# Norm factors formed in rows and spread over the partitions through DRAM

## The chip, the cores and the metric

The kernel runs on one core of a Trainium2 chip. The metric is the device time of one execution in microseconds (us). The kernel before takes 2180.92 us, the median of three runs. The profile shows five engines: TensorE (PE, with its weight loads shown apart as PEld), VectorE (DVE), ScalarE (ACT), GpSimd (POOL), and SyncE (SP), whose queue issues the transfers (SPq).

## The reference

A decoder trunk of two layers on one sequence of 1024 positions and width 1024. Every sub-layer is preceded by an RMS norm, `y = x * rsqrt(mean(x*x) + eps) * g`, and followed by a residual addition:

```
for layer in (0, 1):
    hn = rms_norm(h, mix_norm[layer])
    h = h + (rg_lru_block(hn, ...) if layer == 0 else stick_breaking_attention(hn, w_qkv, w_o))
    h = h + swiglu_ffn(rms_norm(h, ffn_norm[layer]), ffn_w_in[layer], ffn_w_out[layer])
return rms_norm(h, final_norm)

swiglu_ffn(x):  gu = x @ w_in;  (silu(gu[:, :2816]) * gu[:, 2816:]) @ w_out
```

The attention has 16 heads of 64: scores z = q k / 8, from them weights by a suffix product of sigmoids, then weights times v. All is float32; a product is formed of a high and a low part of each operand (fp32r), in three matmuls.

## The kernel before, in words

**Layout.** The activations stand transposed: channels on the partitions (8 blocks `d` of 128), positions along the rows in two halves `n` of 512. `h[d][n]` is the residual, 128x512. The norm's factor belongs to a position, so it is the same on all partitions and differs along the row. It is not applied to the activations ahead of a matmul but to its result: the projections run on `h * g`, and the result is multiplied with the factors where it leaves PSUM. So the factors are needed in the form [128, 512] per half, the same row on every partition.

**Forming the factors.** The squares of h are added over the blocks d into `acc[0]` and `acc[1]` (128x512 each; in the attention into `rbc[0]`, `rbc[1]`), by `squares` (L212: ACT squares, POOL or DVE adds). What is left is the sum over partitions, the root, and the spreading. Before, `stats_mm` (L952) does it for a feed-forward block: for every 128 positions a matmul with the squares as stationary operand and a column of ones as moving one, which puts the sums of 128 positions into one column of `half(ob, 1)`, 128x8 in all; then `rstd` (L178: one ACT root, five DVE instructions on 128x8) into `rcol`. `factors` (L965) spreads them: for every 128 positions a matmul whose stationary operand is the column of `rcol`, broadcast, and whose moving one is the identity, 128x128 each, into the PSUM tile `ob`. One such float32 matmul is two PE instructions in the profile. The attention does the same by halves with `stats` (L202) and `broadcast_r` (L188), and copies the result to `rbc[n]`.

**The feed-forward block** (`mix_out_ffn_in`, L629). The mixer's output projection adds into h; meanwhile the seven operands of a Strassen-like product are formed (`v_steps`, `v_last`). The input projection then runs in steps of 128 channels f; step f needs seven products `i`, in the order 0, 1, 2, 3, 4, 6, 5 (`ORDER`), each 12 matmuls of 128x512. Step 0 is written apart: six products without their last block (L924), the last blocks of these one after another (L926 on, k = 0 to 5), then product 6. Then come the steps f = 1 to 21 in one loop (L1122, `s_` = 0, 1, ...), k counting the seven products. After every product its result is evacuated (`post`) and a piece of the weight work for the next step is issued: a step's weights are the parts `wa` (products 0, 1), `wb` (2, 4), `wc` (3, 5), `wd` (6), each with a high half cast by ACT (`a_hi` L708, `b_hi` L717, `c_hi`, `d_hi`) and a low half by DVE (`a_lo` L712, `b_lo` L721, `c_lo`, `d_lo`); `wb` comes from sums `sb` that DVE forms (L695 to L704). A step's `b_lo` is issued at the start of that step, after the gate of the step before.

`gate` multiplies a step's result with `ob` on DVE (L889), takes Silu on ACT (L891), multiplies again (L893) and with the other branch (L895). The gate of step 0 runs at k = 5 and 6 of `s_` = 0, so `ob` must hold the factors by then.

The last four squares of h are left over when step 0 begins. Before, they run after k = 0 and k = 1 of `s_` = 0, two each, with the adds on DVE (L1172); `stats_mm` follows at k = 3, `factors` at k = 5.

**The attention** starts with the q, k and v columns of the first pair of heads. `qkv_steps` (L1415) gives 3 matmuls at a time; the loop at L1637 counts them (i = 1 to 34), and the table `between` (L1629) says what is put after which: sums of squares of half 0 at 12 and of half 1 at 16, spreading at 17 and 21, and `waiting[0]`, `waiting[1]`, the evacuation of the two q halves, at 18 and 22. `evacuate` (L1445) multiplies with `rbc[n]` on DVE (`t`, L1459), splits into `two` (ACT L1467, DVE L1468; two buffers), and SP spreads it to the tiles `q` (L1471, L1472) and `kk` (L1475) by four transfers. After i = 34 the chunks begin: `z_part` (L1508, two banks in `psZ`), then the sigmoid on ACT that frees the bank (L1521).

**Order.** In both places the order on PE, ACT, DVE and POOL is the order of the program text (`manual_schedule`). In the attention's part that holds for SP too; in the feed-forward block SP's order is the planner's. Every engine runs its list in order: what stands behind a waiting instruction waits as well.

Of the kernel before, what the change touches and what calls it, by code (L numbers as in the profile page):

```python
# [8 lines left out]
F32 = mybir.dt.float32  # L9
# [3 lines left out]
AF = mybir.ActivationFunctionType  # L13
ALU = mybir.AluOpType
PSUM = bass.MemoryType.PSUM

P = 128
S = 1024
D = 1024
ND = D // P  # L20
NT = S // P
# [12 lines left out]
def trunk(  # L34
# [59 lines left out]
    nc.gpsimd.memset(ones, 1.0)  # L94
    eps4 = cp.tile([P, 1], F32, name="eps4")
    nc.gpsimd.memset(eps4, 0.25 * EPS)
    vc = cp.tile([P, P], F32, name="vc")

    rbc = [cp.tile([P, NB], F32, name=f"rbc{n}") for n in range(NH)]
# [7 lines left out]
            for d in range(ND):  # L107
                x_[d] = [xp.tile([P, NB], F32R, name=f"{nm}{d}_{n}") for n in range(NH)]
    rcol = cp.tile([P, NT], F32, name="rcol")
    cp.tile([P, 136], F32, name="edge_l")  # L110


    def load_raw(src, shape):
# [64 lines left out]
    def rstd(dst, sums):  # L178
        n = dst.shape[-1]
        quarter, root = (cp.tile([P, max(n, 4)], F32, tag=x, name=x, bufs=2)[:, 0:n] for x in ("rs_m", "rs_s"))  # L180
        nc.scalar.activation(root, sums, AF.Sqrt, scale=0.25 / D, bias=eps4)
        nc.vector.tensor_scalar(quarter, sums, 0.25 / D, 0.25 * EPS, op0=ALU.mult, op1=ALU.add)
        nc.vector.reciprocal(dst, root)
        nc.vector.tensor_mul(quarter, quarter, dst)
        nc.vector.tensor_add(quarter, quarter, root)
        nc.vector.reciprocal(dst, quarter)

    def broadcast_r(ps_pool, tag, n):  # L188
        ps = ps_pool.tile([P, NB], F32, tag=tag, name="rb_ps")
        for i in range(4):  # L190
            b = 4 * n + i
            nc.tensor.matmul(
                ps[:, i * P : (i + 1) * P],
                lhsT=rcol[:, b : b + 1].broadcast_to([P, P]),
                rhs=ident,
                start=True,
                stop=True,
            )
        nc.vector.tensor_copy(rbc[n], ps)


    def stats(acc, ps_pool, tag, n, i0=0, i1=4):  # L202
        ps = ps_pool.tile([P, NB], F32, tag=tag, name="st_ps")
        accs = acc if isinstance(acc, tuple) else (acc,)
        for i in range(i0, i1):
            for a in accs:
                nc.tensor.matmul(
                    ps[:, i : i + 1], lhsT=a[:, i * P : (i + 1) * P], rhs=ones, start=a is accs[0], stop=a is accs[-1]
                )
        rstd(rcol[:, 4 * n + i0 : 4 * n + i1], ps[:, i0:i1])  # L210

    def squares(h, d, n, sqp, acc, eng=None, first=None):  # L212
        if d == 0 if first is None else first:
            nc.scalar.square(acc[n], h[d][n])
        else:
            sq = sqp[n % len(sqp)] if isinstance(sqp, list) else sqp.tile([P, NB], F32, tag="sq", name="sq", bufs=2)
            nc.scalar.square(sq, h[d][n])
            (eng or nc.gpsimd).tensor_add(acc[n], acc[n], sq)
# [410 lines left out]
    def mix_out_ffn_in(h, mix, bias, layer, gnext, outs):  # L629
# [141 lines left out]
        with tc.manual_schedule(engines={E.PE, E.Activation, E.DVE, E.Pool}):  # L771
# [154 lines left out]
            for k, i in enumerate(ORDER0[:6]):  # L926
                part(P0[i], w, i, rhs_in[i], (HK - 1,))
                if k == 1:
                    w.d_hi()
                    w.d_lo()  # L930
                elif k == 3:
                    nw.a_hi()
                elif k == 5:
                    nw.a_lo()
                if k < 5:
                    post0(i, P0[i])
# [12 lines left out]
            nw.ready = True  # L949


            def stats_mm():  # L952
                st_ps = half(ob, 1)
                for n in range(NH):
                    for i in range(4):
                        nc.tensor.matmul(
                            st_ps[:, 4 * n + i : 4 * n + i + 1],
                            lhsT=acc[n][:, i * P : (i + 1) * P],
                            rhs=ones,
                            start=True,  # L960
                            stop=True,
                        )
                rstd(rcol, st_ps[:, 0:NT])

            def factors():  # L965
                for b in range(NT):
                    nc.tensor.matmul(
                        ob[:, b * P : (b + 1) * P],
                        lhsT=rcol[:, b : b + 1].broadcast_to([P, P]),
                        rhs=ident,  # L970
                        start=True,
                        stop=True,
                    )


            VISITS = (
# [145 lines left out]
            for s_, (kind, x) in enumerate(steps):  # L1122
# [21 lines left out]
                for k, i in enumerate(ORDER):  # L1144
# [22 lines left out]
                        for dn in old:  # L1167
                            finished(*dn)
                    if s_ == 0:
                        if k < 2:  # L1170
                            for _ in range(2):
                                squares(h, *sq_todo.pop(0), rbc, acc, V)  # L1172
                        elif k == 3:
                            stats_mm()
                        elif k == 5:
                            factors()
# [189 lines left out]
    with ExitStack() as st:  # L1366
# [48 lines left out]
        def qkv_steps(q):  # L1415
            for which in range(3):
                w, at = wq.pop((q, which)), 3 * q + which + 1
                if at < 3 * NP:
                    wq[divmod(at, 3)] = next_weights(raws.pop(at))
                else:  # L1420
                    mix[0].w[mix[0].order[0]] = next_weights(mix[0].raw.pop(0))
                for i in (at + 1,) if at < 3 * NP else (at + 1, at + 2):
                    load_link(i)

                ks = (1, 5, 2, 6, 3, 7, 0, 4) if (q, which) == (0, 0) else range(ND)
                for n in range(NH):
                    pool, tag = (psZ, "z") if (q, which) == (0, 0) else (psQ, "qk")
                    ps = pool.tile([P, NB], F32, tag=tag, name="qk_ps")
                    for i, k in enumerate(ks):
                        mm3(ps, w[0][:, k], w[1][:, k], xh[k][n], xl[k][n], i == 0, i == ND - 1)  # L1430
                        if i == 5 and late:
                            late.pop()()
                        if i < ND - 1:
                            yield
                    ev = evacuate(q, which, n, ps)
                    if (q, which) == (0, 0):
                        waiting.append(ev)
                        yield
                    else:
                        next(ev)  # L1440
                        yield
                        next(ev, None)
# [181 lines left out]
        with tc.manual_schedule(engines={E.PE, E.Activation, E.DVE, E.Pool, E.SP}):  # L1624


            load_link(1)
            first = qkv_steps(0)
            between = {  # L1629
                12: lambda: stats(rbc[0], psO, "o", 0),  # L1630
                16: lambda: stats(rbc[1], psO, "o", 1),
                17: lambda: broadcast_r(psO, "o", 0),
                18: lambda: [*waiting[0]],
                21: lambda: broadcast_r(psO, "o", 1),
                22: lambda: [*waiting[1]],
            }
            for i in range(1, 2 * ND * NH + 3):  # L1637
                next(first)
                if i in between:
                    between[i]()  # L1640
                if i > 4 and later:
                    later.pop(0)()

            gains = [len(units) - x for x in (31, 29, 27)]

            last_two, out_work = len(units) - 2 * 12, out_fill()
            amount = {x: 2 for x in (-1, 0, 1, 9, 10, 11, 12)}
            amount.update({x: 1 for x in range(14, 21)})
            c = 0
            for u in range(-LEAD, len(units)):  # L1650
                some = chunks[c : c + 1]
                c += 1
                for a in some:
                    z = z_part(*a)
                if 0 <= u + 2 < len(units):
                    ready[u + 2] = t_split(t_part(*units[u + 2]), *units[u + 2])
                for a in some:
                    z_rest(z, *a)
                if u - last_two == 1:
                    late.pop()()  # L1660
                if u - last_two == 9:
                    mix[0].w[mix[0].order[1]] = next_weights(mix[0].raw.pop(1), nc.gpsimd)
                if later:
                    later.pop(0)()
                for _ in range(2):
                    next(fill, None)
                for _ in range(amount.get(u - last_two, 0)):
                    next(out_work)
                if u in gains:
                    z_rest(z_part(*chunks[c]), *chunks[c])  # L1670
                    c += 1
                if u >= 0:
                    av_part(ready.pop(u), *units[u])
            while later:
                later.pop(0)()
# [48 lines left out]
```

## Time and profile before

| what | us |
|---|---|
| median of the runs | 2180.92 |
| lowest and highest of 3 runs | 2179.82, 2181.77 |
| span of the profiled execution, first to last instruction | 2179.1 |
| PE busy | 2165.8 |
| DVE busy | 1701.4 |
| ACT busy | 1079.8 |
| POOL busy | 113.5 |

The profile gives the profiled execution only as its span; the runs' times lie 0.7 to 2.7 above it. TensorE's granted clock is 1.000 over the span.

In a timeline row the first number is the start in us from the span's start, the second the duration, then engine, line of the kernel, operation, out<-in and the shape of the output; x16 says that 16 instructions stand in one row; brackets give the idle time of the engine before the row and what ended it. In the rows of a line or tile the three numbers behind the count are the shortest, median and longest duration in ns. In the rows of transfers the last number is the us from issue to landing. Consecutive instructions overlap by 0.05 to 0.1 us in their recorded times, and a matmul's recorded duration holds its way through the array: its price is the distance from one start to the next.

### The profile page before, as it was taken

To read this page: it belongs to the slowest core of one execution; us is meant where nothing else is said; L and a number is where in the kernel's file an instruction comes from. 1 tells how busy PE (TensorE), PEld (TensorE's weight loads), DVE (VectorE), ACT (ScalarE), POOL (GpSimd) and SP (SyncE) were. 2 spreads that over 40 slices of the span, in tenths; PEclk is the share of its full clock that TensorE was granted. 3 is DMA by queue.
4 is the path that set the end of the run, shared out by engine and by line. 5 is a ranking of instruction groups with operands and counts; after the bars stand their busy time and mean duration, and the time that the engine had idled before them with its cause. 6 is when DMAs were issued, how large, how long until landed. Compare 5 with 4: busy or idle time off the path is not lost.

```text
span 2179.1 us, 27430 instructions
## 1 busy us (share of the span) xinstructions
PE 2165.8 (99%) x10126; PEld 1802.7 (83%) x10126; DVE 1701.4 (78%) x2380; ACT 1079.8 (50%) x1765; POOL 113.5 (5%) x85
## 2 busy tenths in 40 slices
PE   9999999999999999999999999999999999999998
PEld 7888888888888888888888888888888888888887
DVE  7888777767777887887888888886877777788886
ACT  6677445434444544564555555553543444454556
POOL 1222020000000000000000000002000000000002
PEclk9999999999999999999999999999999999999999
DMA  7111412344444764434333344552133444467452
GB/s 233 49 49 39 135 39 73 102 126 157 138 146 139 247 222 130 145 120 101 100 96 94 95 105 107 143 194 60 52 115 122 147 145 141 144 229 234 138 153 92
DMA packets 296101, 277.64 MB, mean 127 GB/s; under 512 B 15256, under 2 KB 210976, under 8 KB 295968
## 3 DMA queue, kind: packets, MB, share of 16 engines
q1 hardware_dynamic: 295808, 275.64, 40.8%
q8 instruction: 79, 1.29, 0.2%
q14 instruction: 54, 0.44, 0.1%
q10 hardware_dynamic: 160, 0.27, 0.0%
HBM read 175.71 MB, written 74.97 MB: 115 GB/s over the span
## 4 chain that ended last, share of the span: by engine, by line
PE 90%; DVE 6%; ACT 3%; DMA 1%; issue 1%; SPq 0%; DVEq 0%; ACTq 0%
PE p_ps L145 18%; PE p_ps L143 18%; PE p_ps L144 18%; PE qk_ps L143 4%; PE qk_ps L145 4%; PE qk_ps L144 4%; PE wt_ps L1538 3%; PE ob_ps L143 3%; PE ob_ps L144 2%; PE ob_ps L145 2%; PE z_ps L1508 2%; PE z_ps L1509 2%; PE av_ps L1560 2%; PE av_ps L1559 1%; PE a_ps L144 1%; PE a_ps L145 1%
## 5 line engine op out<-in xcount | busy, mean ns | idle before, releaser
L145 PE MATMUL p_ps<-vh,wal 128*128 128x512 f32 x524 | 204.1, 389 | 0.1
L143 PE MATMUL p_ps<-vh,wch 128*128 128x512 f32 x524 | 204.2, 390 | 0.0
L145 PE MATMUL p_ps<-vh,wbl 128*128 128x512 f32 x524 | 204.1, 390 | 0.0
L145 PE MATMUL p_ps<-vh,wcl 128*128 128x512 f32 x524 | 204.1, 390 | 0.0
L143 PE MATMUL p_ps<-vh,wbh 128*128 128x512 f32 x524 | 204.1, 390 | 0.0
L144 PE MATMUL p_ps<-vl,wbh 128*128 128x512 f32 x524 | 203.9, 389 | 0.0
L144 PE MATMUL p_ps<-vl,wch 128*128 128x512 f32 x524 | 203.9, 389 | 0.0
L143 PE MATMUL p_ps<-vh,wah 128*128 128x512 f32 x524 | 203.9, 389 | 0.0
L144 PE MATMUL p_ps<-vl,wah 128*128 128x512 f32 x524 | 203.9, 389 | 0.0
L1547 ACT CAST th<-wt_ps 128x512 fp32r<-128x512 f32 x192 | 92.5, 482 | 209.0 <-PE wt_ps L1538 208.8
L717 ACT CAST wbh<-sb 128x1024 fp32r<-128x1024 f32 (+2 forms) x69 | 69.8, 1011 | 192.9 <-DVE sb L701 192.9
L1548 DVE TENSOR_TENSOR tl<-wt_ps,th 128x512 fp32r<-128x512 f32 x192 | 106.0, 552 | 63.0 <-ACT th L1547 61.2
L143 PE MATMUL qk_ps<-vh,whi 128*128 128x512 f32 x264 | 118.3, 448 | 0.0
L145 PEld LDWEIGHTS p_ps<-vh,wbl 128*128 128x128 f32 x524 | 98.4, 188 | 21.4 <-DVE wbl L721 1.0
L145 PEld LDWEIGHTS p_ps<-vh,wal 128*128 128x128 f32 x524 | 98.3, 188 | 21.4 <-DVE wal L712 1.0
L145 PEld LDWEIGHTS p_ps<-vh,wcl 128*128 128x128 f32 x524 | 98.4, 188 | 21.0 <-DVE wcl L731 0.6
L143 PEld LDWEIGHTS p_ps<-vh,wch 128*128 128x128 f32 x524 | 98.4, 188 | 20.5 <-ACT tb L1106 0.2
L144 PEld LDWEIGHTS p_ps<-vl,wah 128*128 128x128 f32 x524 | 98.4, 188 | 20.4
L144 PEld LDWEIGHTS p_ps<-vl,wbh 128*128 128x128 f32 x524 | 98.4, 188 | 20.4
L144 PEld LDWEIGHTS p_ps<-vl,wch 128*128 128x128 f32 x524 | 98.4, 188 | 20.4
L143 PEld LDWEIGHTS p_ps<-vh,wah 128*128 128x128 f32 x524 | 98.4, 188 | 20.4
L143 PEld LDWEIGHTS p_ps<-vh,wbh 128*128 128x128 f32 x524 | 98.4, 188 | 20.2
(356 smaller groups left out, 5574.1 us busy)
## 6 DMA issues: line engine op xcount, KB each, us to landing
raw<-in_ffn_w_in SPq DMA_DIRECT2D x88, 512.0 KB, 3.9
vl<-pd SPq DMA_DIRECT2D x128, 256.0 KB, 3.9
pd<-U SPq DMA_DIRECT2D x90, 256.0 KB, 2.3
kk<-two SPq DMA_DIRECT2D x64, 256.0 KB, 3.9
raw<-in_ffn_w_out SPq DMA_DIRECT2D x56, 256.0 KB, 3.5
raw<-in_attn_w_qkv SPq DMA_DIRECT2D x24, 512.0 KB, 4.0
q<-two SPq DMA_DIRECT2D x64, 128.0 KB, 2.3
raw<-in_lru_w_in SPq DMA_DIRECT2D x15, 512.0 KB, 3.9
```

The lines of the kernel that those rows point to most:

```text
L143: nc.tensor.matmul(ps, lhsT=wh, rhs=mh, start=first, stop=False, **kw)
L144: nc.tensor.matmul(ps, lhsT=wh, rhs=ml, start=False, stop=False, **kw)
L145: nc.tensor.matmul(ps, lhsT=wl, rhs=mh, start=False, stop=last, **kw)
L717: nc.scalar.copy(self.full(self.wb), self.full(self.sb))
L1508: nc.tensor.matmul(ps[:, 0 : c1 - c0], lhsT=lhsT, rhs=KK[q][hx][:, 0, c0:c1], start=True, stop=False)
L1509: nc.tensor.matmul(ps[:, 0 : c1 - c0], lhsT=lhsT, rhs=KK[q][hx][:, 1, c0:c1], start=False, stop=True)
L1538: nc.tensor.transpose(tp[:, c : c + P], W[q, hx, j, kb // 4][:, (kb % 4) * P : (kb % 4 + 1) * P], ident)
L1547: nc.scalar.copy(th[:, q0:], tp[:, q0:])
L1548: nc.vector.tensor_sub(tl[:, q0:], tp[:, q0:], f32(th)[:, q0:])
L1559: nc.tensor.matmul(ps[:, q0:], lhsT=VV[q][:, kb, hx], rhs=th[:, q0:], start=first, stop=False)
L1560: nc.tensor.matmul(ps[:, q0:], lhsT=VV[q][:, kb, hx], rhs=tl[:, q0:], start=False, stop=last)
```

## The change

`row_stats` forms the sums as rows: a matmul per 128 positions with a stationary operand of eight columns, of which column b is ones and the others zero (cut out of `pick`), and the squares as the moving operand. All add up in one 8x128 area of PSUM (4x128 in the attention), row b holding the 128 sums of block b. The root and the five DVE instructions then work on 8x128, and SP writes the result to DRAM. `row_back` reads 512 factors of it back, the same to all 128 partitions. In the feed-forward blocks `factors` is then two ACT copies from `rbc[n]` to `ob` and no matmul.

Places: the last four squares of a feed-forward block move to k = 3 of step 0's last blocks, behind `a_hi`, with the adds on POOL and `rbc[0]`, `rbc[1]` as buffers in turn; the sums move from k = 3 to k = 1 of `s_` = 0, and the writing and reading back are issued with them. In the attention only the second half changes: the sums stay at 16, the reading back is at 19, and `waiting[1]` moves from 22 to 29. `edge_l` shrinks by what `pick` takes.

```
+    pick = cp.tile([P, 2 * NT], F32, name="pick")
+    nc.gpsimd.memset(pick, 0.0)
+    nc.gpsimd.memset(pick[:, NT : NT + 1], 1.0)
...
+    def row_stats(accs, ps, scratch, back, b0=0):
+        nb = 4 * len(accs)
+        for b in range(nb):
+            nc.tensor.matmul(
+                ps[0:nb, 0:P],
+                lhsT=pick[:, NT - b : NT - b + nb],
+                rhs=accs[b // 4][:, b % 4 * P : (b % 4 + 1) * P],
+                start=b == 0,
+                stop=b == nb - 1,
+            )
+        sums = ps[0:nb, 0:P]
+        quarter, root, r = (scratch[0:nb, i * P : (i + 1) * P] for i in range(3))
+        nc.scalar.activation(root, sums, AF.Sqrt, scale=0.25 / D, bias=eps4[0:nb])
+        nc.vector.tensor_scalar(quarter, sums, 0.25 / D, 0.25 * EPS, op0=ALU.mult, op1=ALU.add)
+        nc.vector.reciprocal(r, root)
+        nc.vector.tensor_mul(quarter, quarter, r)
+        nc.vector.tensor_add(quarter, quarter, root)
+        nc.vector.reciprocal(r, quarter)
+        nc.sync.dma_start(back[b0 : b0 + nb], r)
+
+    def row_back(dst, back, n):
+        nc.sync.dma_start(dst, back[4 * n : 4 * n + 4].rearrange("b c -> (b c)").partition_broadcast(P))
...
                 elif k == 3:
                     nw.a_hi()
+                    while sq_todo:
+                        squares(h, *sq_todo.pop(0), rbc, acc)
...
+            back = dp.tile([NT, P], F32, name=f"back{layer}")
+
             def stats_mm():
-                st_ps = half(ob, 1)
+                row_stats(acc, half(ob, 1), rbc[0], back)
                 for n in range(NH):
-                    for i in range(4):
-                        nc.tensor.matmul(
-                            st_ps[:, 4 * n + i : 4 * n + i + 1],
-                            lhsT=acc[n][:, i * P : (i + 1) * P],
-                            rhs=ones,
-                            start=True,
-                            stop=True,
-                        )
-                rstd(rcol, st_ps[:, 0:NT])
+                    row_back(rbc[n], back, n)
 
             def factors():
-                for b in range(NT):
-                    nc.tensor.matmul(
-                        ob[:, b * P : (b + 1) * P],
-                        lhsT=rcol[:, b : b + 1].broadcast_to([P, P]),
-                        rhs=ident,
-                        start=True,
-                        stop=True,
-                    )
+                for n in range(NH):
+                    nc.scalar.copy(half(ob, n), rbc[n])
...
                     if s_ == 0:
-                        if k < 2:
-                            for _ in range(2):
-                                squares(h, *sq_todo.pop(0), rbc, acc, V)
-                        elif k == 3:
+                        if k == 1:
                             stats_mm()
                         elif k == 5:
                             factors()
...
+            back = dp.tile([4, P], F32, name="back")
+            scratch = ap.tile([P, NB], F32, tag="oo", name="rows", bufs=2)
             between = {
                 12: lambda: stats(rbc[0], psO, "o", 0),
-                16: lambda: stats(rbc[1], psO, "o", 1),
+                16: lambda: row_stats((rbc[1],), psO.tile([P, NB], F32, tag="o", name="st_ps"), scratch, back),
                 17: lambda: broadcast_r(psO, "o", 0),
                 18: lambda: [*waiting[0]],
-                21: lambda: broadcast_r(psO, "o", 1),
-                22: lambda: [*waiting[1]],
+                19: lambda: row_back(rbc[1], back, 0),
+                29: lambda: [*waiting[1]],
             }
```

More of the change, by code (lines that the diff above doesn't have):

```diff
@@ L109, in trunk @@
     rcol = cp.tile([P, NT], F32, name="rcol")
-    cp.tile([P, 136], F32, name="edge_l")
+    cp.tile([P, 120], F32, name="edge_l")
     def load_raw(src, shape):
```

## The prediction

> **What bounds the kernel now.** The page comes first: how busy each engine is, and the chain that ended last.
>
> ```profile
> PE 2165.8 (99%) x10126; PEld 1802.7 (83%) x10126; DVE 1701.4 (78%) x2380; ACT 1079.8 (50%) x1765; POOL 113.5 (5%) x85
> ...
> PE 90%; DVE 6%; ACT 3%; DMA 1%; issue 1%; SPq 0%; DVEq 0%; ACTq 0%
> ```
>
> TensorE (PE) is the bound almost everywhere, so an instruction taken from PE is a gain if nothing else is late at that place. A plain fp32r matmul of 128x512 begins every 0.227 us; a product of the feed-forward block is 12 of them, 2.72 us. I then read the timeline of PE around the two edits of the first block.
>
> ```profile
> 354.78 1.84 PE L956 MATMUL ob<-ones,acc 128*128 128x1 f32 x16
> ...
> 361.84 0.39 PE L145 MATMUL p_ps<-vh,wd 128*128 128x512 f32 x1
> 362.06 1.95 PE L967 MATMUL ob<-ident,rcol 128*128 128x128 f32 x16
> ...
> 364.08 0.39 PE L144 MATMUL p_ps<-vl,wch 128*128 128x512 f32 x1
> L967 PE MATMUL ob<-ident,rcol x32: 271/275/275, 362.1 to 1568.4; 128*128 128x128 f32 x32
> ```
>
> From 361.84 to 364.08 is 2.24 us for two ordinary steps (0.45), so the 16 instructions of L967 cost PE **1.79 us**, and in the second block as much (32 in all). The 16 of L956 cost the same. What PE waits for nearby decides the rest: one weight half arrives late, just where the squares will move.
>
> ```profile
> 343.76 0.39 PE L144 MATMUL p_ps<-vl,wah 128*128 128x512 f32 x1
> 344.21 0.50 PE L145 MATMUL p_ps<-vh,wal 128*128 128x512 f32 x1
> 338.62 1.06 ACT L708 CAST wah<-raw 128x1024 fp32r<-128x1024 f32 x1
> 342.94 1.22 DVE L712 TENSOR_TENSOR wal<-raw,wah 128x1024 fp32r<-128x1024 f32 x1
> 1543.21 1.06 ACT L708 CAST wah<-raw 128x1024 fp32r<-128x1024 f32 x1
> 1547.54 1.22 DVE L712 TENSOR_TENSOR wal<-raw,wah 128x1024 fp32r<-128x1024 f32 x1
> ```
>
> PE goes on 0.45 us after 343.76, not 0.227: it waits until L712 on VectorE (DVE) ends at 344.16. The second block has the same distance from L708 to L712 (4.33 us against 4.32), so I work the first and count it twice.
>
> **Part 1: the factor matmuls go (L967).** Gain on PE: 1.79 us a block. What is late next? These are the weight parts of the following step and the chain that leads to them.
>
> ```profile
> 359.54 0.59 ACT L879 COPY U<-p_ps 128x512 f32<-128x512 f32 x1 [2.40 <-PE p_ps L145]
> 360.17 0.69 DVE L880 TENSOR_TENSOR U<-U 128x512 f32<-128x512 f32 x1 [1.52 <-ACT U L879]
> 363.23 1.05 ACT L717 CAST wbh<-sb 128x1024 fp32r<-128x1024 f32 x1 [3.10 <-DVE sb L701]
> 364.30 1.28 ACT L891 ACT_TABLE_LOAD   x1
> 364.31 1.22 DVE L889 TENSOR_TENSOR G<-ob,G 128x1024 f32<-128x1024 f32 x1
> 366.69 1.22 DVE L893 TENSOR_TENSOR G<-ob,G 128x1024 f32<-128x1024 f32 x1 [1.16 <-ACT G L891]
> 370.95 1.22 DVE L721 TENSOR_TENSOR wbl<-sb,wbh 128x1024 fp32r<-128x1024 f32 x1
> 372.27 0.19 PEld L145 LDWEIGHTS p_ps<-vh,wbl 128*128 128x128 f32 x1
> ```
>
> The chain starts when PE ends the fifth product (k = 4): ACT's copy L879, then DVE from 360.17 to 372.17 without a gap but the 1.16 us in which it waits for Silu. Its last member, L721, makes wbl. PE loads wbl at 372.27, and a load follows its producer by 0.05 us (344.16 to 344.21), so the slack is **0.05 us**. The five product times and the factors between k = 4 and that load fill PE's side; without the factors PE is there 1.79 us sooner and waits 1.74. DVE's list behind L880 is the same in the changed kernel, and the four adds that leave DVE stood before its idle 1.52 us. So this part nets -0.05 us a block, unless the end of k = 4 itself moves.
>
> **Part 2: the row sums (for L956) and their place.** They stand after k = 1 instead of k = 3, still ahead of k = 4, so only their price counts. Sixteen instructions again, now with 128 moving columns and 8 stationary ones. Upper end: L967 also moves 128 columns, and with a load of 128, so 1.79. Lower end: if the load of 128 columns is what sets its step of 0.112 us, 8 columns leave perhaps half, -0.9 us a block. I take 1.79, a difference of 0: an instruction of L967 lasts 0.275 us, as long as the fp32r ones of 128x256 (0.28), and 256 columns move in 256/512 x 0.227 = 0.113 us, which is all of the step. [...]
>
> **Part 3: the last four squares.** They move from after the first two products (ACT square, DVE add) to right behind L708, with the adds on GpSimd (POOL). PE's part is nil, ACT's is moved, DVE loses four adds. But POOL and DVE get in each other's way:
>
> ```profile
> 318.90 0.63 ACT L217 ACTIVATE rbc<-h 128x512 f32<-128x512 f32 x1
> 319.61 1.29 POOL L218 TENSOR_TENSOR acc<-acc,rbc 128x512 f32<-128x512 f32 x1 [1.81 <-ACT rbc L217]
> 319.25 0.75 DVE L799 SCALAR_TENSOR_TENSOR h<-ob_ps,vc,h 128x512 f32<-128x512 f32 x1 [0.91 <-PE ob_ps L145]
> 319.92 2.07 DVE L721 TENSOR_TENSOR wbl<-sb,wbh 128x1024 fp32r<-128x1024 f32 x1
> ```
>
> While POOL adds, a DVE instruction with two SBUF inputs (L721) takes 2.07 us instead of 1.22: it ends 1.09 us after POOL does. L799, with a PSUM input, keeps its 0.75. The moved squares begin about 339.6 (L708's end less the 0.1 by which ACT's instructions overlap). POOL starts 0.71 us after a square does: adds at 340.3, 341.6 and 342.9, each 1.29 long; the third square, into the first one's buffer, waits for the first add and is done in time. DVE reads PSUM in that stretch, until L712 at 342.94, with two SBUF inputs. POOL's third add is ahead by 0.05 to 0.15 us, so L712 ends at 344.2 + 1.09 = 345.3 instead of 344.16, and PE, which has no slack there, waits **1.1 us** longer. The end of k = 4 moves by as much. The fourth add then delays the b parts by another 1.2 us, but the row sums now lie between k = 1 and k = 2 and cover that with their 1.79.
>
> [...]
>
> **Part 4: the way through DRAM.** On DVE five small instructions, on ACT the same root with its table load, on SP's queue one write and two reads per block, on ACT two copies into PSUM.
>
> ```profile
> 352.01 0.69 DVE L873 TENSOR_TENSOR G<-p_ps,G 128x512 f32<-128x512 f32 x1
> 357.18 0.17 DVE L182 TENSOR_SCALAR rs_m<-ob 128x8 f32<-128x8 f32 x1 [2.67 <-ACT rs_s L181]
> vl<-pd SPq DMA_DIRECT2D x128, 256.0 KB, 3.9
> q<-two SPq DMA_DIRECT2D x64, 128.0 KB, 2.3
> ```
>
> [...] The five instructions on 128 columns lie between 0.17 and 0.69 us each; I take 0.32, near the small ones: factors ready at 355.2. The write (4 KB) takes at most the 2.3 of q<-two; each read lands 256 KB, 3.9 as vl<-pd does, the second issued 0.5 later: 361.9. Two ACT copies of 0.59 end at 363.0. They stand in front of L717, which needs ACT at 363.23 + 1.1 = 364.3. So they are hidden by 1.3 us. Behind them ACT has no slack: table load, Silu and L893 follow L717 without a gap. On SP the raw weight loads queue behind the transfers; the next of them waits anyway for a buffer that is free only as L889 starts.
>
> **Part 5: the attention's second half.** Eight broadcast instructions leave PE, and one DVE copy (L199); the write, the read and the evacuation of the second q half take new places.
>
> ```profile
> 974.99 1.05 PE L192 MATMUL rb_ps<-ident,rcol 128*128 128x128 f32 x8
> 977.73 0.39 PE L145 MATMUL qk_ps<-vh,wlo 128*128 128x512 f32 x1
> 985.97 0.35 PE L1508 MATMUL z_ps<-kk,q 128*128 128x256 f32 x1 [1.05 <-DMA kk<-two]
> 989.27 0.33 PE L1508 MATMUL z_ps<-kk,q 128*128 128x384 f32 x1
> 979.11 0.69 DVE L1459 TENSOR_TENSOR t<-qk_ps,rbc 128x512 f32<-128x512 f32 x1
> 984.37 0.62 ACT L1467 CAST two<-t 128x512 fp32r<-128x512 f32 x1 [3.88 <-DVE t L1459]
> 986.04 1.28 ACT L1521 ACT_TABLE_LOAD   x1
> 981.24 7.75 SPq L1475 DMA_DIRECT2D kk<-two  x8
> L1475 SPq DMA_DIRECT2D kk<-two x4: 607/662/1280, 981.2 to 983.3; - x4
> DMA to landing us min/median/max: 3.9/3.9/3.9
> ```
>
> PE gains 0.90 (half of L967's block). The first half of k is then evacuated ahead of the second q half: its t starts at 977.3 (PE's end 978.1 - 0.9, and the way to DVE) instead of 979.11, its transfers at 979.45 instead of 981.24. The second lands by 984.0, as PE arrives (the read of the factors goes ahead of them on SP, behind the first q half; it lands by about 982, and on DVE only the second q half and the later k half stand behind that wait), and the 1.05 us of waiting goes: the first z starts 1.9 us sooner. The second q half's four transfers now follow the first k half's; their first reader is the fifth chunk, five steps on. What is late next: `two` has two buffers, and in the new order the second k half takes the buffer of the first. The fourth of its transfers, issued at 981.5, lands at 985.4; L1467 (984.37 before) waits for it, 1.05 us later than it ran, and behind it on ACT are two casts, the table load and the first sigmoid. That sigmoid ends at 986.04 + 1.05 + 1.28 + 0.28 = 988.7 and frees the bank of the third z (989.27 before). Net **-0.5 us**, between -1.9 (no such wait) and +0.4 (0.9 more of landing).
>
> **The sum.** Per block -1.79 + 1.74 + 1.1 = +1.05, twice +2.1; attention -0.5; together +1.6 on the profiled span of 2179.1, which lies 1.8 below the median of the runs: 2180.9 + 1.6 = **2182.5**. The two new memsets on POOL lie before its long first idle and cost nothing. A measurement of this kernel tells about 0.2% (4.4 us) from no change.
>
> **Rivals.**
> [...]
> - Cheap row sums: half the price, ahead of k = 4, so it counts: 2182.5 - 1.8 = 2180.7. Against it: 0.113 of moving time.
> - All removed PE work counts, as the change seems to say: -3.6 and -1.9 give 2175.4. Against it: wbl's 0.05 us of slack.
> - Slower, the transfers come late. Point of decision: copies done after 364.3 in the block's time, so reads landing after 363.2. From there each microsecond costs one per block, as ACT sits in front of L717. Two late: 2186.5. At the far end SP's planner puts the transfers behind the next raw load, free at 364.3: about 9 us a block, 2200.
>
> **How the numbers follow.** Forecast 0.38; DVE first 0.22; cheap row sums 0.12; all counts 0.11; late transfers 0.17. Range 2176 to 2187: it leaves out the end of "all counts" and the far end of "late". Faster by over 0.2% (below 2176.6): 0.15, from "all counts" and from two small gains meeting; slower (above 2185.3): 0.17; within: 0.68.
>
> **What would show it.** Right: L712 stretched to over 2 us in both blocks with PE waiting for wal about 1.3 us; no factor matmuls, yet PE waiting 1.7 us for wbl in the step after; z waiting for the sigmoid rather than for kk. Wrong: wal unchanged; no wait for wbl; ACT idle in front of the two copies past 364; row sums well under 1.8 us.

## The result and the profile after

The changed kernel takes 2188.04 us (median of 8 runs, 2186.0 to 2188.79), the kernel before 2180.81 beside it (8 runs): a ratio of 1.0032, 95% interval 1.0022 to 1.0042, so 7.2 us slower. The forecast was +1.6, with 2176 to 2187 as its range; the measured time lies above it. The profiled execution spans 2186.2 us, 7.1 more than before. The page first (busy time, share of the span and instructions of each engine).

```profile
PE 2164.4 (99%) x10086; PEld 1797.4 (82%) x10086; DVE 1706.0 (78%) x2371; ACT 1080.0 (49%) x1769; POOL 124.5 (6%) x95
```

The 40 matmuls are gone (10126 before), and PE's busy time fell by 1.4 us; the span grew by 7.1 all the same, so PE stands idle where it did not. Its waits say for what (line waited for: us in total, times, the longest).

```profile
PE p_ps L148 <- DVE wbl L747: 3.0, 3, 1.4
...
PE p_ps L148 <- DVE wal L738: 2.3, 2, 1.1
PE z_ps L1521 <- ACT w L1534: 2.2, 1, 2.2
...
PE ob L218 <- DVE G L890: 1.7, 2, 0.8
```

None of these was among the waits before. Three come in both feed-forward blocks (wbl once more, with 0.23, near the end), the z line once, in the attention. To price them I cut the span at PE instructions that both kernels have. A block's cut goes from the first `ob<-vh,wd` of step 0's last product to the first matmul with `wbl` in the step after the factors; the attention's from its first sums of squares to the fifth z.

| stretch of the span, us | before | after | difference |
|---|---|---|---|
| start | 340.81 | 340.54 | -0.27 |
| block 1 | 31.69 | 33.59 | **+1.90** |
| to the attention's sums | 593.64 | 593.80 | +0.16 |
| attention | 26.67 | 29.43 | **+2.76** |
| to block 2 | 552.59 | 552.59 | 0.00 |
| block 2 | 31.73 | 33.62 | **+1.89** |
| to the end | 601.97 | 602.63 | +0.66 |

The forecast had +1.05 for a block and -0.5 for the attention. The two outer stretches vary among the profiles below by about as much (start 339.5 to 342.3, end 602.1 to 602.8), in kernels without the change there too, so I leave them.

**The block after.** Timelines of PE, DVE, POOL, ACT and SP (start, duration, engine, line; in brackets the idle time before the row and what ended it).

```profile
343.48 0.39 PE L147 MATMUL p_ps<-vl,wah 128*128 128x512 f32 x1
345.00 0.50 PE L148 MATMUL p_ps<-vh,wal 128*128 128x512 f32 x1 [1.13 <-DVE wal L738]
...
349.89 0.39 PE L148 MATMUL p_ps<-vh,wal 128*128 128x512 f32 x1
351.12 1.91 PE L218 MATMUL ob<-acc,pick 128*8 128x128 f32 x16 [0.84 <-DVE G L890]
352.96 0.50 PE L146 MATMUL p_ps<-vh,wbh 128*128 128x512 f32 x1
```

```profile
342.67 2.28 DVE L738 TENSOR_TENSOR wal<-raw,wah 128x1024 fp32r<-128x1024 f32 x1
344.87 1.78 DVE L721 TENSOR_TENSOR s<-raw 128x512 f32<-128x512 f32 x1
...
350.29 0.68 DVE L890 TENSOR_TENSOR G<-G,ob 128x512 f32<-128x512 f32 x1
```

```profile
340.06 6.03 POOL L244 TENSOR_TENSOR acc<-acc,rbc 128x512 f32<-128x512 f32 x4 [17.19 <-ACT rbc L243]
```

In the kernel before, the second and third of DVE's rows stood thus:

```profile
344.08 0.69 DVE L695 TENSOR_TENSOR s<-raw 128x512 f32<-128x512 f32 x1
...
348.41 0.68 DVE L864 TENSOR_TENSOR G<-G,ob 128x512 f32<-128x512 f32 x1
```

The four adds hold POOL from 340.06 to 346.09; the last of them is itself stretched, to 2.27 us from 1.30. DVE's first two instructions with two SBUF inputs in that time are stretched, L738 to 2.28 (1.22 before) and L721 to 1.78 (0.69): 2.15 us lost. PE meets that twice. It waits for wal, 1.29 us from its due place (343.71) to 345.00, and then for L890, the last evacuation of step 0, which ran at 348.41 before: 2.15 later, after the 0.27 by which this span is ahead. L890 reads one half of `ob`; the row sums write the other, and start only when it is done: 350.12 was their due place, 351.12 their start. The next rows show what follows from there.

```profile
372.36 0.39 PE L147 MATMUL p_ps<-vl,wbh 128*128 128x512 f32 x1
374.13 0.50 PE L148 MATMUL p_ps<-vh,wbl 128*128 128x512 f32 x1 [1.38 <-DVE wbl L747]
```

```profile
354.99 0.93 DVE L229 RECIPROCAL rbc<-rbc 8x128 f32<-8x128 f32 x1
...
356.58 0.94 DVE L232 RECIPROCAL rbc<-rbc 8x128 f32<-8x128 f32 x1
...
362.07 0.69 DVE L906 TENSOR_TENSOR U<-U 128x512 f32<-128x512 f32 x1 [3.41 <-ACT U L905]
...
372.86 1.21 DVE L747 TENSOR_TENSOR wbl<-sb,wbh 128x1024 fp32r<-128x1024 f32 x1
```

```profile
361.45 0.59 ACT L905 COPY U<-p_ps 128x512 f32<-128x512 f32 x1 [2.13 <-PE p_ps L148]
362.16 1.21 ACT L989 COPY ob<-rbc 128x512 f32<-128x512 f32 x2
365.13 1.05 ACT L743 CAST wbh<-sb 128x1024 fp32r<-128x1024 f32 x1 [1.76 <-DVE sb L727]
```

```profile
357.55 0.30 SPq L233 DMA_DIRECT2D back<-rbc  x1
358.83 0.82 SPq L236 DMA_DIRECT2D rbc<-back  x2
```

From L905 to L747's end are 12.62 us, as before (359.54 to 372.17, 12.63): the chain has neither grown nor shrunk, and the time that PE saved on the factors it now spends waiting for wbl. The way through DRAM is done in time: the copies end at 363.37, and ACT then idles 1.76 us until L743.

**The attention after.** SP's issues of kk (shortest, median and longest in ns, then the starts of the first and the last), ACT, and PE with the granted clock (columns of the windows: stretch, its length, busy time and instructions of PE, PEld, DVE, ACT, POOL, then PEclk, DMA share, GB/s).

```profile
L1488 SPq DMA_DIRECT2D kk<-two x4: 608/734/1169, 981.8 to 984.0; - x4
```

```profile
988.83 0.62 ACT L1480 CAST two<-t 128x512 fp32r<-128x512 f32 x1 [3.44 <-DMA kk<-two]
...
990.51 1.28 ACT L1534 ACT_TABLE_LOAD   x1
991.80 0.55 ACT L1534 ACTIVATE w<-z_ps 128x128 f32<-128x128 f32 x2
```

```profile
989.55 0.39 PE L148 MATMUL qk_ps<-xg,wlo 128*128 128x512 f32 x1
992.14 0.69 PE L1521 MATMUL z_ps<-kk,q 128*128 128x384 f32 x1 [2.20 <-ACT w L1534]
...
995.50 0.44 PE L1521 MATMUL z_ps<-kk,q 128*128 128x512 f32 x1
```

```profile
992.00:993.00 1.00, 0.86 (x3) 0.87 (x4) 0.82 (x2) 0.35 (x2) 0.00 (x0) 0.58 0.94 203
993.00:994.00 1.00, 1.00 (x4) 0.81 (x3) 1.00 (x3) 0.49 (x1) 0.00 (x0) 0.50 0.96 197
994.00:995.00 1.00, 1.00 (x3) 0.79 (x3) 0.66 (x1) 0.00 (x0) 0.00 (x0) 0.50 0.98 279
```

The wait that I forecast is there, and is longer: the cast L1480 needs a buffer of `two` whose transfer, issued as the fourth at 984.0, lands at 988.8. Behind it on ACT stand two casts, the table load and the first sigmoid, which frees the bank for the third z. PE stands still for 2.2 us, and when it goes on, its clock is halved: from 992 to 996 the granted shares are 0.58, 0.50, 0.50 and 0.72, short of full by 1.70 us, which is 3.4 us at half rate. Matmuls of 128x512 then last 0.63 us instead of 0.39. From the third z to the fourth are 3.36 us; before, the fourth came 1.73 after the third (989.27), so the clock alone takes **1.6 us**.

```profile
991.00 0.39 PE L1508 MATMUL z_ps<-kk,q 128*128 128x512 f32 x1
```

### The profile page after: what moved, and what is told of

The parts are those of the page before. It is cut to its first block, busy times and chain, and to the rows that moved or that the text cites. A ratio compares the mean times of both kernels' runs of the same rounds, so it can differ in the third digit from the quotient of the medians.

```text
span 2186.2 us, 27378 instructions
## 1 busy us (share of the span) xinstructions
PE 2164.4 (99%) x10086; PEld 1797.4 (82%) x10086; DVE 1706.0 (78%) x2371; ACT 1080.0 (49%) x1769; POOL 124.5 (6%) x95
## 3 DMA queue, kind: packets, MB, share of 16 engines
q8 instruction: 79, 1.29, 0.2%
## 4 chain that ended last, share of the span: by engine, by line
PE 94%; DVE 3%; ACT 2%; issue 0%; DMA 0%; SPq 0%; DVEq 0%; ACTq 0%
PE p_ps L148 18%; PE p_ps L146 18%; PE p_ps L147 18%; PE qk_ps L146 4%; PE qk_ps L148 4%; PE qk_ps L147 4%; PE wt_ps L1551 3%; PE a_ps L147 3%; PE a_ps L148 3%; PE a_ps L146 3%; PE ob_ps L147 2%; PE ob_ps L146 2%; PE ob_ps L148 2%; PE z_ps L1521 2%; PE z_ps L1522 2%; PE av_ps L1573 2%
## 5 line engine op out<-in xcount | busy, mean ns | idle before, releaser
L743 ACT CAST wbh<-sb 128x1024 fp32r<-128x1024 f32 (+2 forms) x69 | 69.6, 1009 | 187.9 <-DVE sb L727 187.9
```

What stands on the lines that cost most here:

```text
L743: nc.scalar.copy(self.full(self.wb), self.full(self.sb))
```

## The experiments

The theory that these profiles give has three parts. (A) In a block the chain from the end of k = 4 to wbl takes back whatever PE saves, so a block pays just what delays k = 4. (B) Two things delay it, both from POOL's adds: wal, 1.0 us, and the row sums behind L890, 0.9. (C) In the attention the wait for `two` and the lost clock make +2.7. The rivals: the transfers through DRAM are late, or the new rows themselves cost, in which case mending the adds gains nothing.

**The two halves of the change alone.** The first kernel has the attention as before:

```
             between = {
                 12: lambda: stats(rbc[0], psO, "o", 0),
-                16: lambda: row_stats((rbc[1],), ..., scratch, back),
+                16: lambda: stats(rbc[1], psO, "o", 1),
...
-                19: lambda: row_back(rbc[1], back, 0),
-                29: lambda: [*waiting[1]],
+                21: lambda: broadcast_r(psO, "o", 1),
+                22: lambda: [*waiting[1]],
```

> The change in the two feed-forward blocks alone; the attention as before. Theory: each block loses about 2.1 us (PE reaches the load of wbl in the step after at 374.13 in the changed kernel against 372.27, and 0.28 had been gained at the start), in two parts: wal late by 1.1 (POOL's third add holds L738 back) and the row sums late by 1.1 (they wait for L890 on ob). So +4.3 us over the kernel before, with those two waits in both blocks. Rival, as in the prediction: only the 1.1 us of wal count, +2.1 us, and the rest of the loss belongs to the attention.

Measured: 2184.87 us, a ratio of 1.0018 (1.0009 to 1.0027), which is +3.9; blocks +1.93 and +1.88, attention +0.09. The second has the feed-forward blocks as before and the attention changed.

> The change in the attention alone; the feed-forward blocks as before. Theory: +2.7 us over the kernel before: the first z about 1.4 us sooner relative to its surroundings, then the third z late by 2.2 us of waiting for the first sigmoid, because the cast of the second k half waits for the first k half's last transfer, then half the granted clock for about 3 us, 1.6 us more. Rival, as in the prediction: -0.5 us; then what the changed kernel shows there comes from the feed-forward block in front of it.

Measured: 2182.72 us, 1.0008 (0.9998 to 1.0017); blocks -0.01 and 0.00, attention +2.62. The times alone don't tell this from no change; the stretch does. Its PE and its clock:

```profile
989.85 0.44 PE L1534 MATMUL z_ps<-kk,q 128*128 128x384 f32 x1 [1.91 <-ACT w L1547]
```

```profile
990.00:991.00 1.00, 1.00 (x5) 0.91 (x6) 1.00 (x3) 0.56 (x2) 0.00 (x0) 0.91 0.99 205
991.00:992.00 1.00, 1.00 (x4) 0.71 (x4) 1.00 (x2) 0.00 (x0) 0.00 (x0) 0.50 0.94 199
```

The same wait and the same halved clock: PE runs at the full clock for about 1 us after the wait, then loses 1.7 us between 990 and 995, 3.4 us at half rate as in the whole change. So the losses stand side by side: two blocks +3.8, attention +2.6, against +6.55 in the three stretches of the whole change.

**The row sums in a PSUM bank of their own**, attention as before:

```
-                row_stats(acc, half(ob, 1), rbc[0], back)
+                row_stats(acc, pp.tile([P, NB], F32, tag="p", name="sums_ps"), rbc[0], back)
```

> As the run with the feed-forward change alone, but the row sums go to a PSUM tile of their own out of the ring of six, not into ob. Theory: the wait of the row sums for L890 goes, the one for wal stays: +2.1 us over the kernel before, half of what the feed-forward change alone loses. Rival: the row sums are late for another reason (the fourth add on POOL, or the operands), and nothing changes: +4.3 us.

Measured: 2183.03 us, 1.0007 (0.9998 to 1.0017); blocks +1.00 and +0.96. PE has no wait left for L890, and the other two stay:

```profile
343.98 0.50 PE L148 MATMUL p_ps<-vh,wal 128*128 128x512 f32 x1 [1.13 <-DVE wal L738]
```

```profile
372.20 0.50 PE L148 MATMUL p_ps<-vh,wbl 128*128 128x512 f32 x1 [1.38 <-DVE wbl L747]
```

So the wait for L890 is worth 0.9 a block, and half of the loss goes with it.

**The adds on DVE**, behind L738, on top of that:

```
                 elif k == 3:
                     nw.a_hi()
-                    while sq_todo:
-                        squares(h, *sq_todo.pop(0), rbc, acc)
+                    for d, n in sq_todo[0:2]:
+                        nc.scalar.square(rbc[n], h[d][n])
                 elif k == 5:
                     nw.a_lo()
+                    for d, n in sq_todo[0:2]:
+                        V.tensor_add(acc[n], acc[n], rbc[n])
+                    del sq_todo[0:2]
+                    while sq_todo:
+                        squares(h, *sq_todo.pop(0), rbc, acc, V)
```

> As the run with a PSUM tile of their own for the row sums, but the four adds of squares run on DVE, behind the low part of wa, so POOL does nothing there. Theory of the prediction's chain: both waits are gone, 1.8 us of PE work per block is gone too, and still nothing is gained, because PE then waits 1.7 us for wbl in the step after: 0 us against the kernel before (-0.5 to +0.5). Rival: removed PE work counts once nothing else is late: -3.6 us.

Measured: 2182.56 us, 1.0002 (0.9993 to 1.0011); blocks +0.11 and +0.04. On DVE, L738 is back at its 1.22, and wbl is waited for as before:

```profile
343.39 1.22 DVE L738 TENSOR_TENSOR wal<-raw,wah 128x1024 fp32r<-128x1024 f32 x1
...
351.45 0.68 DVE L890 TENSOR_TENSOR G<-G,ob 128x512 f32<-128x512 f32 x1
```

```profile
373.06 0.50 PE L148 MATMUL p_ps<-vh,wbl 128*128 128x512 f32 x1 [1.38 <-DVE wbl L747]
```

This is parts A and B at once. The two delays together were the whole loss of a block; and with both gone, 1.79 us less work on PE gains nothing, since PE waits for wbl. It takes both mends: with the adds on DVE, L890 ends no sooner (352.13), while the row sums begin at 349.89, so in `ob` they would have waited for it by some 2.2 us (an estimate from these two times; no run has the adds on DVE and the sums in `ob`). Had the way through DRAM been late, the loss would have stayed.

**Two DVE instructions exchanged**, on top of that: in the step after the factors the low half of wb is formed ahead of the second gate.

```
-                if gf is not None and s_:
+                if gf is not None and s_ > 1:
                     gate(gf, 0)
                 if not w.ready:
                     w.b_lo()
                     if kind == "f":
                         w.c_hi()
+                if gf is not None and s_ == 1:
+                    gate(gf, 0)
```

> As the run with the four adds on DVE and a PSUM tile of their own for the row sums; besides, in the first step after (s_ = 1) the low part of wb is issued ahead of the first gate multiplication, so DVE makes wbl 1.1 us sooner. Theory of the chain: PE's wait for wbl shrinks from 1.8 to 0.7 us in both blocks, and so much of the removed factor matmuls becomes a gain: -2.2 us against the kernel before. Rival: wbl is only the first of several things late by 1.8 us there, and the next one takes the wait over: 0 us.

Measured: 2180.14 us, 0.9994 (0.9985 to 1.0003); blocks -1.07 and -1.11.

```profile
369.71 1.22 DVE L747 TENSOR_TENSOR wbl<-sb,wbh 128x1024 fp32r<-128x1024 f32 x1
370.84 1.22 DVE L915 TENSOR_TENSOR G<-ob,G 128x1024 f32<-128x1024 f32 x1
```

```profile
370.98 0.50 PE L148 MATMUL p_ps<-vh,wbl 128*128 128x512 f32 x1 [0.25 <-DVE wbl L747]
```

One instruction with a step of 1.13 is out of the chain, and 1.1 us of the saved matmuls count. The times alone don't tell this from no change; the stretches do.

**The attention: a buffer of its own for the second q half**, feed-forward blocks as before:

```
-                two = ap.tile([P, 2, NB], F32R, tag="two", name="two", bufs=2)
+                if (q, which, n) == (0, 0, 1):
+                    t0, t1 = (ap.tile([P, NB], F32R, tag=x, name=x, bufs=3) for x in ("th", "tl"))
+                else:
+                    two = ap.tile([P, 2, NB], F32R, tag="two", name="two", bufs=2)
+                    t0, t1 = two[:, 0], two[:, 1]
...
```

> The change in the attention alone, but the second q half is split into two buffers of its own (th and tl, idle at that time), so the second k half no longer takes the buffer of the first. Theory: its cast runs about 1.6 us sooner, the third z waits 0.3 us instead of 1.9 for the first sigmoid, PE does not idle long enough to lose its clock, and the attention gains: -0.9 us against the kernel before. Rival: the cast is late because the factors come back late (DVE waits for them), and the time stays at +1.5 to +2.7 us.

Measured: 2181.34 us, 1.0000 (0.9991 to 1.0009). The attention's stretch is at -0.81, as the theory has it, with neither the third z's wait nor the halved clock. But the time did not move: the stretch behind it, to block 2, is 553.68 instead of 552.59, **+1.09**. The offset between the two traces grows evenly there, so it is no single wait. The groups of PE's instructions between 1000 and 1541 us, sorted by shape, show where (count | busy, mean ns | idle):

```profile
L1589 PE MATMUL av_ps<-th,v 128*128 128x512 f32 x96 | 38.7, 403 | 0.0
```

All widths together, of this kernel and then of the kernel before:

```profile
L1589 PE MATMUL av_ps<-th,v 128*128 128x512 f32 x192 | 66.8, 348 | 0.0
```

```profile
L1559 PE MATMUL av_ps<-th,v 128*128 128x512 f32 x192 | 65.7, 342 | 0.0
```

No wait, but 192 matmuls of the weighted sums, each some 6 ns longer: 1.1 us. They read th, whose tag the spare buffer shares.

**The weight load ahead of the row write**, feed-forward blocks as before. After the change a 512 KB load of weights stood on SP right behind the row write; here it is issued three places earlier, and no longer at its old place:

```
+                13: lambda: load_link(3),
                 16: lambda: row_stats(...
```

> The change in the attention alone, but the raw weights that stand behind the row write on SP (512 KB) are issued ahead of it. Theory: the transfers of the first k half no longer share the queue's engines with them and land about 1 us sooner; the third z waits 1 us or less for the first sigmoid, and the granted clock may stay: between +0.1 and +1.7 us against the kernel before. Rival: these transfers are late because they are issued late (two long reciprocals on DVE), and nothing changes: +2.7 us in the trace.

Measured: 2183.18 us, 1.0010 (1.0001 to 1.0019); attention +1.02. Against the attention alone the stretch is 1.6 shorter, but that is not the load's doing:

```profile
987.47 0.62 ACT L1494 CAST two<-t 128x512 fp32r<-128x512 f32 x1 [3.19 <-DMA kk<-two]
```

```profile
990.77 0.44 PE L1535 MATMUL z_ps<-kk,q 128*128 128x384 f32 x1 [1.97 <-ACT w L1548]
```

```profile
991.00:992.00 1.00, 1.00 (x6) 0.87 (x6) 1.00 (x3) 0.49 (x1) 0.00 (x0) 1.00 0.96 201
```

The third z starts 24.05 us after the stretch's beginning, and 24.03 in the attention alone: the place of the load is worth nothing. What went is the halved clock, after a wait of the same length (1.97 us here, 1.91 in the attention alone). So the load as the cause of the late transfers falls, and the clock's 1.6 us show as a term of their own. Each kernel has one profile, and the medians of the runs do not show this gain (1.0010 here, 1.0008 in the attention alone): how often the clock falls in the other runs is not shown.

**All mends together**: row sums in their own bank, adds on DVE, exchange, own buffers, early load.

> The whole change with all the mends: adds on DVE, a PSUM tile of their own for the row sums, wbl ahead of the first gate, the second q half's own buffers, the weights ahead of the row write. Theory: the terms add up, -2.2 and about -1.2: -3.4 us against the kernel before. Rival: the attention's start then meets another wait, and only the feed-forward part is left: -2.2 us.

Measured: 2180.02 us, 0.9992 (0.9983 to 1.0001); blocks -1.07 and -1.09, attention -0.85, and again +1.16 behind it.

**The same with other buffers.** In the two kernels with own buffers, these opened the tags th and tl earlier than the weighted sums do. Here they come from a tag that the row sums have opened already:

```
-                    t0, t1 = (ap.tile([P, NB], F32R, tag=x, name=x, bufs=3) for x in ("th", "tl"))
+                    t0, t1 = (ap.tile([P, NB], F32R, tag="oo", name=x, bufs=2) for x in ("q0", "q1"))
```

> The kernel of e9_all with one difference: the second half of the first q pair is split into two buffers of the tag oo, which the row sums have already opened, instead of two that open the tags th and tl before their time. In e6_own_two and e9_all the 96 full-width matmuls of the weighted sums with th took 403 ns each instead of 396, and all 192 took 66.8 us instead of 65.7, which is the 1.1 us by which the rest of the attention grew. Theory: that comes with the early opening of th and tl, so it goes; 396 ns, 65.7 us and a rest of the attention of 552.6 us are expected, with the blocks at -1.1 each and the attention's start at -0.85 as in e9_all, 3 us under the kernel before, a ratio near 0.9986. Rival: the 1.1 us comes with the earlier third sigmoid or with the split itself; then the matmuls stay at 403 ns, the rest of the attention at 553.7 us, and the ratio near 0.9992.

Measured: 2178.79 us (median of 11 runs, 2177.59 to 2179.57) against 2181.84, a ratio of **0.9987 (0.9977 to 0.9996)**. Blocks -1.08 and -1.11, attention -0.82, behind it +0.10. The same group of PE:

```profile
L1584 PE MATMUL av_ps<-th,v 128*128 128x512 f32 x96 | 38.0, 396 | 0.0
```

So the 1.1 us came with the early opening of th and tl, and this version is faster than both kernels: its slowest run lies under the fastest of the kernel before beside it (2180.17). Why the matmuls that read th grow by 7 ns when its tag is opened earlier (another place in SBUF would be a guess) stays open.

## Why the prediction was wrong, step by step

- **The factors' matmuls (part 1): right.** -1.79 on PE, and the chain to wbl, unchanged at 12.6 us, takes it back; the forecast wait of 1.74 is 1.54 (372.59 to 374.13). The kernel with the adds on DVE shows the net at +0.1 and 0.0, against -0.05.
- **The price of the row sums (part 2): right.** 1.84 from 351.12 to 352.96, so the cheap-row-sums rival falls. **Their place: wrong, and this is the first step that failed.** "Only their price counts" overlooked that they write into `ob`, whose other half L890 was still to read; "the row sums ... cover that with their 1.79" used them as cover without asking what they wait for themselves. Price: 0.9 a block, 1.8 in all.
- **POOL's adds against L738 (part 3): right.** L738 is stretched to 2.28 in both blocks, PE idle for 1.29 in block 1 (about 1.3 forecast), 1.0 a block against 1.1. POOL was there first, its third add at 342.58 and 1551.96, L738 at 342.67 and 1552.08: DVE first (L738 ahead of that add), given 0.22, failed by 0.1 us each time, and no run has that order. What I missed is that the second stretch (L721, 1.78) reaches PE too, by L890.
- **The way through DRAM (part 4): right, with wrong sizes.** The two reciprocals took 0.93 and 0.94 us, where I had 0.32 for each of the five; the factors were ready at 357.5 instead of 355.2. The 355.2 counted from 353.6, with an estimate of 2.3 us for what POOL's third and fourth adds take from DVE; measured were 2.15, DVE was past L899 (L873 before) at 353.38, and the first of the five instructions began at 354.78, behind ACT's root. The write and the reads were quicker than my bounds (write issued at 357.55, copies begun at 362.16), so the copies ended at 363.37, 363.0 forecast, 1.76 ahead of L743. The late-transfer rival falls: its time was near, its cause was not there.
- **The attention (part 5): the second step that failed.** The mechanism was right (no wait worth naming for kk, first z earlier by 1.3 of the 1.9, the cast waiting for a buffer of `two`, the third z for the first sigmoid), its size was not. In the trace of after, 1.79 us later at that place, the cast should have begun at 987.2; it began at 988.83, 1.6 later. The fourth transfer's issue makes 0.7 of that (984.0 against 983.3); by the timeline the row instructions, the two reciprocals above all, held DVE ahead of it, which was not tried by itself. The landing makes 0.9 (4.8 us instead of 3.9), which the prediction had as its upper end; why it took longer stays open. And the halved clock, of which I had no term, makes another 1.6: -0.5 + 1.6 + 1.6 = +2.7, measured +2.76.

The sum then: 2 x 0.85 more in the blocks and 3.3 more in the attention are 5.0 of the 5.5 us by which the profiled span missed the forecast; the rest lies in the outer stretches.

The halved clock came after 2.2 us of standstill in the changed kernel (3.4 us at half rate from 992 to 996) and after 1.91 in the attention alone; with the load ahead of the row write PE stood still for 1.97 and kept its clock at 1.00. So the length of the wait alone does not tell, and what does these runs do not show.

## What to carry to other kernels

When a moved instruction serves as cover, ask first what it waits for itself: which tile it writes, and who has still to read any part of it. Work taken from the bounding engine counts only as far as the chain on the next engine is shorter; here it took an exchange of two DVE instructions to turn 1.79 us of saved matmuls into 1.1. And a wait of some 2 us on TensorE cost nearly as much again in clock in two of these traces, 1.6 us, and nothing in a third.

## What the runs showed of the hardware

- A reciprocal on DVE took 0.93 us for 4x128 and for 8x128 alike, where a product of the same tile took 0.28, and 0.17 for 128x4. As rows, the two of a set cost 1.5 us more than as columns.

```profile
970.16 0.17 DVE L186 RECIPROCAL rcol<-rs_s 128x4 f32<-128x4 f32 x1
...
973.41 0.93 DVE L229 RECIPROCAL rows<-rows 4x128 f32<-4x128 f32 x1
974.37 0.28 DVE L230 TENSOR_TENSOR rows<-rows 4x128 f32<-4x128 f32 x1
```

- A stationary operand of 8 columns made a matmul of 128 moving columns no quicker (1.84 us for 16, against 1.79 with 128 columns).
- Two buffers that opened a tag earlier made 192 matmuls that read this tag slower by some 6 ns each, 1.1 us in all, and other buffers in their place did not.
